# High and low parts of the input weights kept in DRAM between the two halves of the tokens

## The chip, the cores and the metric

The kernel runs on one core of one Trainium2 chip. The metric is the device time of one execution in microseconds (us). Smaller is better. A NeuronCore has a matrix engine (TensorE, PE, with its weight loads as PEld), three engines for element-wise work (VectorE DVE, ScalarE ACT, GpSimd POOL), and DMA engines; nearly all DMAs of this kernel are issued on the queue of SyncE (SP).

## The reference

One layer of a hybrid decoder over 1024 prompt tokens and 8 single sample tokens, width 1024. Cut to what matters here:

```python
def parallel_mixer(h, shift0, wkv0, w_in, ...):
    proj = h @ w_in                    # 1024 -> 2816 columns
    z_a = gelu(proj[..., :1024])       # u, v of mixer A (4 heads x 128)
    out_a = chunk_spatial_gate(u, headnorm(v), gm_ws, gm_bs)
    pb, shift_new = token_shift(proj[..., 1024:], shift0, mu)
    r, k, v, wl, al, gl = split(pb)    # mixer B: 8 heads x 64, and three lora inputs
    yb, wkv_new = wkv7_scan(r, decay, k, v, kk, a, wkv0)   # a recurrence over the tokens
    out_b = (headnorm(yb) + bonus) * g
    return concat([out_a, out_b]) @ w_out, ...

def layer(x):
    x = x + parallel_mixer(rmsnorm(x), ...)
    x = x + cross_attn(rmsnorm(x), mem_k, mem_v, w_xq, w_xo)
    x = x + square(relu(rmsnorm(x) @ w_up)) @ w_down
```

Everything is float32. The 2816 columns of `w_in` are 22 blocks of 128 columns.

## The kernel before

**Products.** A float32 product is made of three matmuls in the format fp32r: each operand is split into a high part (the value cast to fp32r) and a low part (the value minus that), and high x high, high x low and low x high are summed in PSUM (`gemm`, L125). `split` (L100) is a cast on ACT (L103) and a subtraction on DVE or POOL (L104).

**First phase.** The mixer runs in two halves of tokens (`hf` 0 and 1): 512 prompt tokens and the 8 sample tokens, then 512 prompt tokens. In each half, every one of the 22 column blocks is projected once: `proj` (L358) loads the 1024 x 128 block as a tile `wst` (512 KB, in rows of 512 bytes; `w_tile`, L109), splits it into `wh` and `wl` (`load_w`, L114), multiplies it with the halves `xh`, `xl` of the normalised x in two blocks of columns, 48 matmuls in all, and scales the result out of PSUM on DVE (L369). So each block of `w_in` is loaded and split twice. The subtraction runs on DVE or POOL by a rule in L361: in the first half 8 on DVE and 14 on POOL, in the second 14 on DVE and 8 on POOL. `rkv`, `loras` (by way of `shifted`) and `proj_a` call `proj`.

The tags `wst`, `wh` and `wl` belong to the pool `wp` (L90) with two buffers each, so a weight tile is loaded at most two projections ahead of its split, and split at most two ahead of its matmuls. `wst` has other users: the x of the second half as it is read and turned (`x_store`, L278), that x again at the start of the second half (`load_x`, L314), the memory tokens (`mem_norm`, `mem_load`) and the weights of all later stages.

Beside the projections the first phase runs the recurrence of mixer B for pairs of heads in chunks of 64 tokens (`decay`, `factors`, `gram`, `inverse`, `join`, `fold`, `chain`, `outs`, `gn`), mixer A (`norm_a`, `mix_a`), the sample tokens, and at its end the keys and values of the memory (`memkv`, 16 weight blocks loaded and split like the others). A list written by hand (`ORDER`, L39) sets the order in which these steps are written down. From it and from a model of the times the compiler sets the order of the instructions on each engine and queue; each engine and queue then takes its own in that order, and waits on semaphores.

**Second phase.** Output projection, cross attention and the feed-forward layer, from about 665 us on. It doesn't use the projections' code.

Of the kernel before, what the change touches and what calls it, by code (L numbers as in the profile page):

```python
# [9 lines left out]
F32 = mybir.dt.float32  # L10
F32R = mybir.dt.float32r
# [8 lines left out]
P = 128  # L20
D = 1024
KT = 8
# [48 lines left out]
class K:  # L71
    ORDER = order()

    def __init__(self, ctx, tc, a, o, phases=9, dbg=None):
        self.ctx, self.tc, self.nc, self.a, self.o = ctx, tc, tc.nc, a, o
        self.dbg = dbg or {}
        nc = self.nc
        self.consts = ctx.enter_context(tc.tile_pool(name="consts", bufs=1))
        self.dr = ctx.enter_context(tc.tile_pool(name="dr", bufs=1, space=DRAM))
        self.cp = ctx.enter_context(ExitStack())  # L80
        self.pg = self.cp.enter_context(tc.tile_pool(name="pg", bufs=2, space=PSUM))
        self.pm = self.cp.enter_context(tc.tile_pool(name="pm", bufs=2, space=PSUM))
        self.d_o = [self.dr.tile([8, P, HALF], F32, name=f"d_o{i}") for i in range(2)]
        self.d_os = self.dr.tile([8, P, NB], F32, name="d_os")
        self.d_x = self.dr.tile([8, P, T], F32, name="d_x")
        self.d_h = self.dr.tile([16, 7, P, HT], F32, name="d_h")
        self.d_m = self.dr.tile([P, KT, NMEM], F32, name="d_m")
        self.d_k = self.dr.tile([8, P, NMEM], F32, name="d_k")
        self.d_v = self.dr.tile([NMEM, D], F32, name="d_v")
        self.wp = ctx.enter_context(tc.tile_pool(name="wp", bufs=2))  # L90
        with ExitStack() as c1:
            self.phase1(c1)
        if phases >= 2:
            self.phase2(phases)
# [141 lines left out]
    def phase1(self, c1):  # L236
        nc, tc = self.nc, self.tc
        self.sb, self.sa, self.xp, self.s1 = (c1.enter_context(tc.tile_pool(name=nm, bufs=1)) for nm in ("sb", "sa", "xp", "s1"))
        self.s2a, self.s2 = (c1.enter_context(tc.tile_pool(name=nm, bufs=2)) for nm in ("s2a", "s2"))
        self.sl = c1.enter_context(tc.tile_pool(name="sl", bufs=1, side="right"))  # L240
        self.pc = c1.enter_context(tc.tile_pool(name="pc", bufs=1, space=PSUM))
        self.py = c1.enter_context(tc.tile_pool(name="py", bufs=2, space=PSUM))
        self.pre, self.prew, self.scales = [], [], []
        first = [t[2] + 12 if t[0] == "loras" else t[2] + 4 * t[3] for t in self.ORDER if t[0] in ("loras", "rkv")]
        for i in range(4):
            xt = (self.sa if i < 2 else self.sb).tile([P, D], F32, tag=("zv", "zv", "pt", "nb")[i], name="xt", bufs=2 if i < 2 else 1)
            nc.sync.dma_start(xt, self.a["x_prompt"][0][i * P:(i + 1) * P, :])
            self.pre.append(xt)
            if i % 2 == 1:
                self.prew.append(self.w_tile(self.a["w_in"][0][:, 1024 + first[i // 2] * P:1024 + (first[i // 2] + 1) * P]))  # L250
        self.ident = self.consts.tile([P, P], F32, name="ident")
        make_identity(nc, self.ident)
        self.g = {}
        self.prm = self.consts.tile([P, 74], F32, name="prm")
        self.params([("norm_mix_g", 8)], self.s1.tile([64, P], F32, tag="xsr", name="prm_g"), 0)
        self.params([("tshift_mu", 14)], self.s1.tile([P, P], F32, tag="strow", name="prm_mu"), 8)
        self.half = ({}, {})
        self.nb = None
        for name, *args in self.ORDER:
            if args and name not in ("memkv", "sample_update"):  # L260
                self.s = self.half[args[0]]
            getattr(self, name)(*args)
# [95 lines left out]
    def proj(self, hf, col0, dst, sdst):  # L358

        nc, tc = self.nc, self.tc  # L360
        w = self.load_w(self.a["w_in"][0][:, col0:col0 + P], st=self.prew.pop(0) if self.prew else None, eng=nc.vector if hf == int(col0 >= 1024) else nc.gpsimd)  # L361
        for b0, b1 in ((0, 256), (256, self.ncols(hf))):
            ps = self.pg.tile([P, 512], F32, tag="g", name="ps_g")
            self.gemm(ps[:, 0:b1 - b0], w, self.s["xh"], self.s["xl"], slice(b0, b1))
            if self.scales:
                self.scales.pop(0)()
            e = min(b1, HALF)
            with tc.high_priority():
                nc.vector.tensor_tensor(dst[:, b0:e], ps[:, 0:e - b0], self.s["rb"][:, b0:e], op=ALU.mult)  # L369
                if b1 > HALF:  # L370
                    nc.vector.tensor_tensor(sdst, ps[:, HALF - b0:b1 - b0], self.s["rb"][:, HALF:], op=ALU.mult)

    def shifted(self, hf, mi, out):

        nc, s1, s2 = self.nc, self.s1, self.s2
        raw = s2.tile([P, HALF + 1], F32, tag="raw", name="raw")
        if hf == 0:
            nc.gpsimd.memset(raw[:, 0:1], 0.0)
        else:
            nc.scalar.copy(raw[:, 0:1], self.carry[:, mi:mi + 1])  # L380
        self.proj(hf, 1024 + mi * P, raw[:, 1:], self.sraw[:, :, mi])
        nc.gpsimd.tensor_copy((self.carry if hf == 0 else self.shp)[:, mi:mi + 1], raw[:, HALF:HALF + 1])
        nc.scalar.activation(out, raw[:, 1:], AF.Copy, scale=self.mu1[:, mi:mi + 1])
        nc.vector.scalar_tensor_tensor(out, raw[:, 0:HALF], self.g["tshift_mu"][:, mi:mi + 1], out, op0=ALU.mult, op1=ALU.add)
# [1278 lines left out]
```

## Time and profile before

| | us |
|---|---|
| median of 3 runs | 1791.45 (1782.59 to 1793.16) |
| the profiled execution, its own time | 1794.84 |
| its span, first to last instruction | 1793.1 |
| PE busy in the span | 1634.6 (91%) |
| DVE, POOL, ACT busy | 1221.3, 837.1, 781.1 |

The profile is of one execution. Busy time is time in which an engine executes something; issuing and waiting are not counted. PE's matmuls are pipelined, and the ends of them are modelled, so that a busy PE may still be below its peak. A wait is put down to the instruction that ended it. L12 is line 12 of the kernel before. The span began with the first instruction, and all times of rows are counted from there.

### The profile page before, as it was taken

What the parts mean: (1) busy time and instruction counts of PE and PEld (TensorE: products, weight loads), DVE (VectorE), ACT (ScalarE), POOL (GpSimd) and SP (SyncE); (2) the same over time, 40 slices, a digit from 0 to 9 for tenths busy, and PEclk for the clock granted to TensorE, in tenths of its full rate; (3) what the DMA queues carried; (4) which work ended last, traced back from release to release, by engine and by line L of the source; (5) the groups of instructions that cost most, each with busy time, mean ns of one, the idle gap of its engine ahead of it and who ended that gap; (6) DMA issues with size and microseconds to landing.
All of it is one profiled execution on the core that took longest, in us unless ns stands there. A gap on an engine that the chain in (4) does not pass through costs nothing. (4 is left out here: it accounts for less than half of the span.)

```text
span 1793.1 us, 38347 instructions
## 1 busy us (share of the span) xinstructions
PE 1634.6 (91%) x15379; PEld 1521.9 (85%) x15379; DVE 1221.3 (68%) x2300; ACT 781.1 (44%) x1467; POOL 837.1 (47%) x643
## 2 busy tenths in 40 slices
PE   6989868998897689998999889999999999999997
PEld 6878757886786578887988789999999989999997
DVE  5586687768757965656667365655655697877796
ACT  4535543455443234433344233444544564444442
POOL 5450152323146864466343178687754533222343
PEclk8999978999898889999999999999999999999998
DMA  4411423221122456555455342567644585555442
GB/s 139 118 37 58 124 69 93 83 57 52 53 76 73 131 172 196 174 169 175 144 184 165 139 130 82 167 201 225 195 155 142 186 281 184 156 142 153 137 125 107
DMA packets 248547, 244.28 MB, mean 136 GB/s; under 512 B 24937, under 2 KB 191233, under 8 KB 248369
## 3 DMA queue, kind: packets, MB, share of 16 engines
q1 hardware_dynamic: 248324, 241.82, 44.1%
q8 instruction: 121, 1.98, 0.5%
q14 instruction: 58, 0.47, 0.1%
q10 hardware_dynamic: 44, 0.01, 0.0%
HBM read 179.95 MB, written 61.83 MB: 135 GB/s over the span
## 5 line engine op out<-in xcount | busy, mean ns | idle before, releaser
L104 POOL TENSOR_TENSOR wl<-wst,wh 128x1024 fp32r<-128x1024 f32 x70 | 170.3, 2433 | 125.6 <-ACT wh L103 112.1
L1215 PE MATMUL ps_S<-c_o,wS 128*128 128x258 f32 x1536 | 226.4, 282 | 0.0
L1215 PE MATMUL ps_S<-c_cb,wS 128*128 128x258 f32 x1536 | 226.0, 282 | 0.0
L136 PE MATMUL ps_g<-xh,wh 128*128 128x256 f32 (+1 forms) x704 | 214.6, 305 | 5.4 <-ACT xr L288 1.8
L136 PE MATMUL ps_g<-xl,wh 128*128 128x256 f32 (+1 forms) x704 | 209.6, 298 | 0.5 <-DVE xl L104 0.5
L136 PE MATMUL ps_g<-xh,wl 128*128 128x256 f32 (+1 forms) x704 | 207.7, 296 | 0.0
L1215 PEld LDWEIGHTS ps_S<-c_cb,wS 128*128 128x128 f32 x1536 | 201.8, 189 | 0.0
L1215 PEld LDWEIGHTS ps_S<-c_o,wS 128*128 128x128 f32 x1536 | 201.8, 189 | 0.0
L136 PE MATMUL ps_g<-o,wh 128*128 128x260 f32 (+1 forms) x768 | 178.0, 325 | 14.5 <-DVE yq L1240 8.9
L1215 PE MATMUL ps_A<-c_cb,wA 128*128 128x258 f32 x1152 | 173.0, 284 | 7.6 <-ACT c_cb L103 3.9
L1215 PE MATMUL ps_A<-c_o,wA 128*128 128x258 f32 x1152 | 172.7, 284 | 0.0
L1215 PEld LDWEIGHTS ps_A<-c_cb,wA 128*128 128x128 f32 x1152 | 153.4, 190 | 8.8 <-ACT c_cb L103 4.3
L1215 PEld LDWEIGHTS ps_A<-c_o,wA 128*128 128x128 f32 x1152 | 153.2, 190 | 0.4 <-DVE c_o L104 0.4
L103 ACT CAST wh<-wst 128x1024 fp32r<-128x1024 f32 x92 | 96.1, 1046 | 130.5 <-PE ps_g L136 63.9
L136 PEld LDWEIGHTS ps_g<-o,wh 128*128 128x128 f32 x768 | 129.2, 191 | 27.6 <-issue 9.2
L136 PEld LDWEIGHTS ps_g<-xh,wh 128*128 128x128 f32 x704 | 140.3, 199 | 12.9 <-issue 5.0
L136 PEld LDWEIGHTS ps_g<-xl,wh 128*128 128x128 f32 x704 | 139.9, 199 | 5.6 <-issue 2.2
L136 PEld LDWEIGHTS ps_g<-xh,wl 128*128 128x128 f32 x704 | 139.2, 198 | 3.0 <-issue 1.4
L1171 POOL TENSOR_TENSOR rS<-wr,rS 128x512 f32<-128x512 f32 x48 | 70.4, 1467 | 121.9 <-DMA wr<-in_w_down_dram 61.7
L136 PE MATMUL ps_g<-o,wl 128*128 128x260 f32 (+1 forms) x384 | 123.5, 322 | 1.4 <-POOL wl L104 1.4
L103 ACT CAST wS<-rS 128x512 fp32r<-128x512 f32 x96 | 59.3, 620 | 144.1 <-POOL rS L1171 84.1
L104 DVE TENSOR_TENSOR wS<-rS,wS 128x512 fp32r<-128x512 f32 x96 | 81.9, 853 | 46.6 <-ACT wS L103 46.3
(493 smaller groups left out, 3877.2 us busy)
## 6 DMA issues: line engine op xcount, KB each, us to landing
hb<-d_h SPq DMA_DIRECT2D x105, 258.0 KB
wst<-in_w_in_dram SPq DMA_DIRECT2D x44, 512.0 KB
d_h<-ht SPq DMA_DIRECT2D x64, 258.0 KB
wr<-in_w_down_dram SPq DMA_DIRECT2D x26, 512.0 KB
d_h<-yq SPq DMA_DIRECT2D x48, 258.0 KB
wst<-in_w_out_dram SPq DMA_DIRECT2D x16, 512.0 KB
ck<-in_cache_mem_k_dram SPq DMA_DIRECT2D x32, 256.0 KB
ck<-in_cache_mem_v_dram SPq DMA_DIRECT2D x32, 256.0 KB
```

Of the source, the lines that this page charges most:

```text
L103: (heng or nc.scalar.copy)(hi, src)
L104: (eng or nc.vector).tensor_tensor(lo, src, hi.bitcast(F32), op=ALU.subtract)
L136: nc.tensor.matmul(ps, l[:, k, :], r[:, cols], start=(k == 0 and i == 0), stop=(k == kt - 1 and i == 2))
L1171: nc.gpsimd.tensor_tensor(R[n], R[x], R[y], op=op)
L1215: nc.tensor.matmul(ps[:, s], l[:, i, :], r[:, c, cols], start=k == 0 and j == 0, stop=k == 3 and j == 2)
```

## The change

In the first half `proj` loads and splits as before, and when the matmuls are written down it stores both halves of the weights, as they stand in SBUF, to a new DRAM tensor `d_w` (22 blocks, high and low, 512 KB each; a partition's 4 KB are one row). In the second half it makes no split: it loads the two halves from `d_w` into tiles `w2`. These take, in turn, the buffers of (`wh`, `wl`), of (`wh`, `wl`) again, and both buffers of `wst`.

```diff
+        self.d_w = self.dr.tile([22, 2, P, KT, P], F32, name="d_w")
...
-        self.pre, self.prew, self.scales = [], [], []
+        self.pre, self.prew, self.scales, self.nw = [], [], [], 0
...
     def proj(self, hf, col0, dst, sdst):
-        w = self.load_w(self.a["w_in"][0][:, col0:col0 + P], st=self.prew.pop(0) if self.prew else None, eng=nc.vector if hf == int(col0 >= 1024) else nc.gpsimd)
+        if hf == 0:
+            w = self.load_w(self.a["w_in"][0][:, col0:col0 + P], st=self.prew.pop(0) if self.prew else None, eng=nc.vector if hf == int(col0 >= 1024) else nc.gpsimd)
+        else:
+            tags = (("wh", "wl"), ("wh", "wl"), ("wst", "wst"))[self.nw % 3]
+            self.nw += 1
+            w = [self.wp.tile([P, KT, P], F32R, tag=tg, name="w2") for tg in tags]
+            for j in range(2):
+                nc.sync.dma_start(w[j].bitcast(F32), self.d_w[col0 // P, j])
...
+        if hf == 0:
+            for j in range(2):
+                nc.sync.dma_start(self.d_w[col0 // P, j], w[j].bitcast(F32))
```

## Rows read from the trace of the kernel before

**Rows 1.** The page's first part: busy us, share of the span, instructions of each engine

```profile
PE 1634.6 (91%) x15379; PEld 1521.9 (85%) x15379; DVE 1221.3 (68%) x2300; ACT 781.1 (44%) x1467; POOL 837.1 (47%) x643
```

**Rows 2.** Stages: length, busy of PE, PEld, DVE, ACT, POOL, clock, DMA share, GB/s

```profile
0.00:310.00 310.00, 257.08 (x3075) 227.27 (x3075) 215.81 (x497) 145.92 (x267) 117.92 (x152) 0.89 0.31 90
310.00:556.00 246.00, 229.65 (x2520) 197.99 (x2520) 176.86 (x437) 117.80 (x230) 78.71 (x67) 0.94 0.21 64
556.00:665.00 109.00, 72.37 (x1190) 63.56 (x1190) 88.37 (x161) 33.94 (x60) 81.55 (x64) 0.80 0.48 139
```

**Rows 3.** PE's waits in 310 to 556: us in total, times, longest

```profile
PE psgate L705 <- ACT y L702: 4.9, 1, 4.9
PE ps_j L584 <- DVE pt L567: 3.6, 1, 3.6
PE psf L624 <- ACT bk L547: 2.3, 1, 2.3
...
PE psz L646 <- ACT bk L626: 1.1, 1, 1.1
```

**Rows 4.** PE's waits in 556 to 665

```profile
PE psgn L700 <- DVE y L671: 10.7, 1, 10.7
PE psf L624 <- DVE y L671: 9.5, 1, 9.5
```

**Rows 5.** Weight splits in 310 to 556: busy us, mean ns, idle before and why

```profile
L103 ACT CAST wh<-wst 128x1024 fp32r<-128x1024 f32 x22 | 23.0, 1045 | 25.8 <-PE ps_g L136 22.4 <-DMA wst<-in_w_in_dram 1.7 <-issue 1.6
L104 DVE TENSOR_TENSOR wl<-wst,wh 128x1024 fp32r<-128x1024 f32 x14 | 18.8, 1340 | 2.2 <-ACT wh L103 2.2
L104 POOL TENSOR_TENSOR wl<-wst,wh 128x1024 fp32r<-128x1024 f32 x8 | 20.2, 2527 | 39.9 <-ACT wh L103 39.9
```

**Rows 6.** Timeline of SP's issues: start us, us, queue, line

```profile
12.11 0.33 SPq L847 DMA_DIRECT2D bsb<-in_gm_bs_dram  x1
...
13.03 0.44 SPq L713 DMA_DIRECT2D strow<-in_state_shift_dram  x1
...
46.16 1.01 SPq L111 DMA_DIRECT2D wst<-in_w_in_dram  x2
...
303.87 3.75 SPq L315 DMA_DIRECT2D xr<-d_x  x2
310.51 9.95 SPq L111 DMA_DIRECT2D wst<-in_w_in_dram  x4
```

**Rows 7.** Timelines of DVE and POOL around the second half's first weight subtraction

```profile
315.18 0.60 DVE L864 TENSOR_SCALAR vn<-vn,bnmv,lnrs 128x128 f32<-128x128 f32 x2
...
316.30 2.56 DVE L864 TENSOR_SCALAR vn<-vn,bnmv,lnrs 128x128 f32<-128x128 f32 x2
...
316.07 2.44 POOL L104 TENSOR_TENSOR wl<-wst,wh 128x1024 fp32r<-128x1024 f32 x1 [7.82 <-ACT wh L103]
```

**Rows 8.** Windows with DMA share and GB/s last; the last: matmuls of L136 alone

```profile
1009.00:1022.00 13.00, 8.60 (x32) 6.93 (x33) 1.95 (x5) 1.21 (x3) 0.74 (x1) 0.87 0.80 296
46.00:60.00 14.00, 13.94 (x107) 12.60 (x106) 6.09 (x16) 7.52 (x11) 6.98 (x9) 1.00 0.52 152
...
46.00:160.00 114.00, 75.57 (x547) 70.39 (x546) 0.94 0.26 75
```

**Rows 9.** Timelines of ACT, POOL and PE: casts, subtractions, matmuls

```profile
37.15 2.00 ACT L103 CAST wh<-wst 128x1024 fp32r<-128x1024 f32 x2 [15.74 <-issue]
50.48 1.06 ACT L103 CAST wh<-wst 128x1024 fp32r<-128x1024 f32 x1
...
308.18 1.33 ACT L106 ACTIVATE xh<-xr,prm 128x512 fp32r<-128x512 f32 x2 [0.94 <-DMA xr<-d_x]
...
38.27 2.35 POOL L104 TENSOR_TENSOR wl<-wst,wh 128x1024 fp32r<-128x1024 f32 x1 [0.37 <-ACT wh L103]
...
48.14 0.28 PE L136 MATMUL ps_g<-xh,wl 128*128 128x264 f32 x1
...
316.69 0.58 PE L136 MATMUL ps_g<-xh,wh 128*128 128x256 f32 x1
```

## What the change was predicted to do

> **What bounds the kernel now.** I read the busy times first: TensorE (PE) is busy 91% of the span, no other engine over 68% [rows 1]. The change touches only the projections, so I cut the span by stage next [rows 2]: first half of the tokens 0 to 310 us, second half 310 to 556, the tail of that half (recurrence, memory keys and values) 556 to 665, the rest after. The reader is to see how little PE idles where the splits are taken away: 246 - 229.65 = 16.4 us in the second half, 109 - 72.37 = 36.6 us in the tail. Then PE's waits in these two stretches [rows 3, 4]. The first names no wait for `wh` or `wl`. It names copies and vector work of the recurrence (4.9 us for an ACTIVATE of `gn`, 3.6 us for `inverse`, 2.3 us for `ends`); the tail's largest, 10.7 and 9.5 us, are for `y` out of `outs`. So the second half is bound by PE's own work, the tail by the recurrence's chain over VectorE (DVE), ScalarE (ACT) and GpSimd (POOL). The splits sit beside both.
>
> **What it removes.** In the second half 22 casts on ACT, 23.0 us; 14 subtractions on DVE, 18.8 us; 8 on POOL, 20.2 us [rows 5]. PE waits for none of them by name, so they don't come off the time one for one. They count only through what stands behind them on in-order engines. I price this by bounds: nothing below; above, all PE idle time of the second half and half that of the tail (the other half stands behind copies of `memkv` and `inverse` that stay), 16.4 + 18.3 = 34.7 us. The removed work is 18.8 of 176.9 us of DVE's time and 23.0 of 117.8 us of ACT's [rows 2, 5], 11 and 20%. I let PE's waits shrink by 15% in the second half, 2.5 us, and by the 11% of DVE in the tail, 4.0 us, since only what arrives earlier can help there. One more place: the first projection of the second half. Its x halves are done early, but its weight tile `wst` shares two buffers with the x loads, so that its load is issued at 310.51, after the last x load [rows 6], and its subtraction runs on POOL from 316.07 to 318.51 [rows 7], while PE begins with the high part at 316.69 and then turns to the recurrence [rows 9]. Read back into `wh` and `wl`, free since the projections before, these weights can be there first: I take 2.0 us, out of the waits of 2.3 and 1.1 us there [rows 3]. Sum of the gains: 8.5 us.
>
> There is a second effect of POOL's subtractions. Beside the one at 316.07 DVE needs 2.56 us for two ops whose like took 0.60 us just before [rows 7]: some 2 us lost. Over 8 subtractions that is at most 16 us of DVE time, which again is off PE's list; by the 11% for 18.8 us it would be worth another 3 us at most. I leave it to the range.
> The Trainium skill, "SBUF — State Buffer", section "Who interferes with whom", states that a VectorE op with two SBUF inputs is blocked for the whole of a GpSimd op that reads SBUF. The trace agrees that DVE is held up, here even for an op with one large input. By that rule the gain would be the 8.5 us and these 3 us, so 11.5 us.
>
> **What it adds in the first half.** 44 stores of 512 KB on SP's queue, 23 MB. An SP issue takes 0.33 to 0.5 us [rows 6]; 44 are about 18 us of a queue that mostly waits. No row shows a store of this shape. The nearest are transfers with rows of 4 KB: a window of them moved 296 GB/s at a share of 0.80 [rows 8], 370 GB/s at full share. So a pair of 1.05 MB needs an estimated 2.8 us, all 22 need 62 us, or 0.20 of the 310 us; the stage's share is 0.31 [rows 2]. There is room on average. At the busiest place, 46 to 60 us, the share is 0.52 [rows 8]; the 107 matmuls there, 48 a projection, are some two projections; they add 2.1 MB, 5.7 us of 14, 0.41: 0.93, tight but below full.
>
> The stores also hold `wh` and `wl`. Each has two buffers, so the cast of projection n+2 waits for the matmuls of n, and now for its stores too. ACT works in order: behind a late cast stand all its copies for the recurrence, and POOL's subtraction, and then PE. The tightest case is the third projection: subtraction done at 38.27 + 2.35 = 40.6, last matmul issued at 48.14 and over at 48.4 [rows 9], so that the stores have 7.8 us to land; the pair needs 2.8 us and the delay of a landing. For that delay an x load gives a bound: it was issued at 303.87 [rows 6] and ended a wait of ACT at 308.18 [rows 9], 4.3 us for 512 KB. 2.8 + 4.3 = 7.1 us is still below 7.8. I price the hold at nothing; its cover is the matmuls, and if that is gone it costs what the rival below says. What I do charge: at 46.16 SP issues two loads at once [rows 6], and the cast at 50.48 follows [rows 9]. The stores of the two projections whose casts run at 37.15 [rows 9] come due at the same time; with half of their 2.1 MB ahead of these loads they land 2.8 us later, and PE has nothing else there. Low end 0, high end 5.7; I take 2.0 us, somewhat less than that delay, since the split that follows ends a little before PE wants it.
>
> **What it moves.** Loads of the second half: 22 of 512 KB become 44 of 512 KB. At 2.8 us a pair [rows 8] that is 62 us of transfer in 246, 0.25, in a stage whose share is 0.21 with the old loads in it [rows 2]. A projection's tiles come free when the one three before it ends; between lie two projections of 48 matmuls, at the 107 matmuls in 14 us of the dense stretch [rows 8] 12.6 us in all, against 7.1 us for a pair to land. Nothing. SP waits now for PE where it waited for the subtraction; behind it stand small loads and `d_o` stores that have no reader near by. The three sets of buffers also hold both `wst` each third time; until `mem_load` nobody else wants them. Nothing.
>
> **Sum.** 8.5 - 2.0 = 6.5 us less. The profiled execution took 1794.8 us (span 1793.1 and 1.7 around it); 1788.3 then. It lies 3.4 us over the median of the runs, 1791.45, so I predict 1785.
>
> **Rivals.**
> *The recurrence is freed.* If the waits in [rows 3, 4] are mostly for engines that the splits held up, the upper bound comes off: 34.7 less 2.0 us, 1759. For it: DVE is busy 88.37 of the tail's 109 us, POOL 81.55 [rows 2]. Against it: the work removed lies before the tail, and the tail's own load stays. 18%.
> *The stores hold the tiles.* Slower. The place is the first half from 46 to 160 us, where 547 matmuls [rows 8], 11 projections, run close together. It decides once a pair lands more than 7.8 us after the subtraction: the share of 0.93 has only to be uneven for that. Price one store late or both, 1.4 to 2.8 us, for each of 11, 15 to 31 us, less 6.5: 1791.45 + 9 to 1791.45 + 24, 1800 to 1816, about 1808. The Trainium skill, "DMA: Bandwidth & Descriptors", section "Anatomy of one DMA", says, of DMAs issued from GpSimd, that a completion waits for the receipt of the write, the longer when the target is HBM; no row here shows a store's landing. 15%.
> *The order is drawn anew.* SP issued a load of `strow` at 13 us [rows 6], whose step, `sample_shift`, stands in the middle of the written list for this half: the order on each queue is set at compile time and not by the text. With 66 more transfers and 44 fewer vector instructions the engines' order can differ anywhere in the first 665 us. One wait like the two of 10 us in the tail more, and the gain is gone: 1791.45 - 6.5 + 10 = 1795, no change. 17%.
> *Forecast*: 50%, itself 1774 to 1797.
>
> **Numbers.** A measurement of this kernel can tell about 1% from no change, 18 us. Faster by more, below 1773.5: the freed recurrence nearly whole and a little of the forecast, 0.20. Slower by more, above 1809.4: not quite half of the held tiles, some of the new order, and what of the forecast's costs I may have missed, 0.13. Within: 0.67. The range is 1760 to 1809: it reaches to the freed recurrence's full price and over the middle of the held tiles, and leaves out about a tenth at each end.
>
> **What would show it.** Right: the cast and subtraction groups in the second half gone; PE's waits in the first half unchanged but for 2 us near 50; the second half ending some 4 us earlier counted from its start, the tail 4 us shorter; no wait of ACT for a DMA on `d_w`. Wrong: ACT or POOL waiting for `d_w` stores in the first half; PE waiting for `w2` loads; the tail shorter by over 15 us, or a wait of PE that isn't in [rows 3, 4].

## The result and the profile after

The changed kernel takes 1804.25 us (median of 7 executions, 1799.04 to 1814.14), the kernel before, run beside it, 1790.79 us (7, 1782.59 to 1793.16): ratio 1.0076, 95% interval 1.0051 to 1.0101. It is 13.5 us slower, inside the predicted range and on the other side of the forecast of 1785.

The profiled execution of the changed kernel was its longest, 1814.14 us, 9.9 us over the median, with a span of 1812.4 us; that of before was 1794.84 us. The two profiles therefore differ by 19.3 us, and the places of the loss below are those of these two executions. From here on lines are those of the changed kernel (L104 of before is L105, L498 is L509, L607 is L618, L816 is L827).

Busy us, share of the span and instructions of each engine, against [rows 1]:

```profile
PE 1649.6 (91%) x15379; PEld 1532.2 (85%) x15379; DVE 1198.9 (66%) x2286; ACT 754.5 (42%) x1442; POOL 806.2 (44%) x635
```

The splits are gone: ACT has 27 us less work, DVE 22, POOL 31. The stages, in the columns of [rows 2]:

```profile
0.00:310.00 310.00, 252.54 (x2961) 222.29 (x2962) 209.07 (x481) 142.15 (x263) 115.21 (x150) 0.88 0.50 165
310.00:556.00 246.00, 234.49 (x2584) 201.07 (x2583) 155.06 (x430) 93.91 (x205) 49.06 (x59) 0.94 0.31 107
556.00:665.00 109.00, 63.61 (x961) 54.18 (x960) 90.41 (x155) 29.19 (x58) 70.27 (x58) 0.75 0.40 118
```

The second half has PE at 234.49 us for 229.65 before: it idles less in this window, as hoped. The tail has 63.61 for 72.37, at a granted clock of 0.75 for 0.80, although ACT and POOL do less there. PE's waits in the tail, against [rows 4]:

```profile
PE ps_j L595 <- DVE pt L578: 12.9, 1, 12.9
PE psgram L509 <- DVE ab L510: 11.8, 1, 11.8
PE ps_kvt L1008 <- DVE kvt L1003: 8.9, 3, 7.4
PE psf L635 <- DVE y L682: 7.0, 1, 7.0
```

The wait of 10.7 us for `y` of before is gone; 12.9 us for the end of `inverse` and 11.8 us for `gram` stand in its place. Place by place, from the first and last matmuls in PE's timeline: the first half's last projection ends 7.1 us later (312.6 for 305.5), the second half's 5.3 us later (561.3 for 556.0), and the last matmul of `join 1 1` 23.8 us later (682.5 for 658.7). So the stretch from the last projection to the end of that join is 18.5 us longer (121.2 for 102.7); some 4 us of it come back later.

Within that stretch two pieces grew most; 3.2 us more stand ahead of them. The *ladder* of `inverse 1 1` is 28 small DVE operations between two transposes, from 607.9 to 634.1 us before (26.3 us) and from 616.4 to 651.1 after (34.7). The *join* behind it, from its first matmul to its last, is 637.9 to 658.7 before (20.8 us) and 654.8 to 682.5 after (27.7). In both kernels the four `sample_update` steps, each of six POOL and three DVE operations and eleven loads, run beside them. The timelines show what they do. First DVE's and POOL's rows in the ladder (start, us, engine, line, tiles), the first of them from the kernel before, where no POOL operation ran beside it:

```profile
633.90 0.21 DVE L564 TENSOR_TENSOR pb<-pb,ptmp 128x28 f32<-128x28 f32 x1
...
644.99 2.27 DVE L575 TENSOR_TENSOR pb<-pb,ptmp 128x72 f32<-128x72 f32 x1
...
649.62 0.20 DVE L574 TENSOR_TENSOR ptmp<-pb 128x28 f32<-128x28 f32 x1
649.85 1.21 DVE L575 TENSOR_TENSOR pb<-pb,ptmp 128x28 f32<-128x28 f32 x1
...
644.82 2.33 POOL L105 TENSOR_TENSOR wl<-wst,wh 128x1024 fp32r<-128x1024 f32 x1
...
649.74 1.26 POOL L826 TENSOR_TENSOR stmp<-sS,sbv 128x512 f32<-128x512 f32 x1 [0.22 <-DMA sbv<-d_sv]
```

The operation that took 0.21 us before takes 1.21 us when it starts just behind a POOL product of 1.26 us, and a larger one of its kind 2.27 us behind a weight subtraction of 2.33. Over 0.9 us took 13 of the 28, and 9 before; every one of these has a POOL operation beside it. All 28 together take 23.3 us, for 16.7 before. Then SP, POOL, DVE and PE in the join:

```profile
659.60 9.25 SPq L815 DMA_DIRECT2D sbv<-d_sv  x8
...
661.45 1.27 POOL L818 TENSOR_TENSOR stmp<-sS,sbv 128x512 f32<-128x512 f32 x1 [10.46 <-DMA sbv<-d_sv]
...
673.71 1.27 POOL L826 TENSOR_TENSOR stmp<-sS,sbv 128x512 f32<-128x512 f32 x1
...
672.07 1.58 PE L616 MATMUL ps_j<-tt,ab 32*32 32x32 f32 x64
...
675.01 0.69 DVE L827 TENSOR_REDUCE sy<-stmp 128x8 f32<-128x512 f32 x1 [6.89 <-POOL stmp L826]
675.73 0.68 DVE L618 COPY wj<-ps_j 32x512 f32<-32x512 f32 x1
...
676.47 0.31 PE L622 MATMUL ps_j<-wj,dt 32*32 32x32 f32 x2 [2.27 <-DVE wj L618]
...
681.32 1.19 PE L622 MATMUL ps_j<-wj,dt 32*32 32x32 f32 x62
```

DVE waits 6.89 us for the last product of the last `sample_update`, whose first product had itself waited 10.46 us for a load, and behind this reduction stands the copy of `wj` that the join needs. In the compiled order of the kernel before the last reduction stands behind all copies of the join; in the changed kernel it stands right in front of that one. The 6.89 us aren't the price, though: what the copy reads, the matmuls of L616, is ready only at 672.07 + 1.58 = 673.65 us. The copy starts at 675.73, so that it is about 2 us late, and PE waits 2.27 us for it. After that PE runs 25 matmuls of `memkv` between the first two and the other 62 of L622; in the kernel before such a block stands ahead of all 64 and runs while the copy is made. From the end of L616 to the end of the join it takes 8.9 us for 4.3 before, from the join's start to there 18.9 for 16.5. So the late copy is some 2 of the join's 6.9 us; the rest lies in the order of PE's matmuls and in its other waits.

### The profile page after: what moved, and what is told of

Read it like the earlier page. It is cut to its first block, busy times and chain, and to the rows that moved or that the text cites. A ratio compares the mean times of both kernels' runs of the same rounds, so it can differ in the third digit from the quotient of the medians.

```text
span 1812.4 us, 38412 instructions
## 1 busy us (share of the span) xinstructions
PE 1649.6 (91%) x15379; PEld 1532.2 (85%) x15379; DVE 1198.9 (66%) x2286; ACT 754.5 (42%) x1442; POOL 806.2 (44%) x635
## 5 line engine op out<-in xcount | busy, mean ns | idle before, releaser
L105 POOL TENSOR_TENSOR wl<-wst,wh 128x1024 fp32r<-128x1024 f32 x62 | 149.3, 2408 | 106.4 <-ACT wh L104 94.5
L137 PE MATMUL ps_g<-xh,w 128*128 128x256 f32 x704 | 148.6, 301 | 1.4 <-DVE raw L377 1.4
L137 PEld LDWEIGHTS ps_g<-xh,w 128*128 128x128 f32 x704 | 116.1, 197 | 8.8 <-issue 3.4
L104 ACT CAST wS<-rS 128x512 fp32r<-128x512 f32 x96 | 59.2, 620 | 145.4 <-POOL rS L1182 85.9
L104 ACT CAST wh<-wst 128x1024 fp32r<-128x1024 f32 x70 | 73.1, 1045 | 111.0 <-PE ps_g L137 63.2
L105 DVE TENSOR_TENSOR wS<-rS,wS 128x512 fp32r<-128x512 f32 x96 | 81.6, 850 | 50.6 <-ACT wS L104 50.4
L137 PE MATMUL ps_g<-xh,wh 128*128 128x256 f32 (+1 forms) x352 | 108.5, 309 | 5.7 <-ACT xr L289 2.2
L137 PE MATMUL ps_g<-xl,wh 128*128 128x256 f32 (+1 forms) x352 | 106.5, 303 | 0.6 <-DVE xl L105 0.5
L137 PE MATMUL ps_g<-xh,wl 128*128 128x256 f32 (+1 forms) x352 | 105.3, 300 | 0.0
L137 PE MATMUL ps_g<-xl,w 128*128 128x256 f32 x352 | 104.8, 298 | 0.0
```

The source lines that it names most:

```text
L104: (heng or nc.scalar.copy)(hi, src)
L105: (eng or nc.vector).tensor_tensor(lo, src, hi.bitcast(F32), op=ALU.subtract)
L137: nc.tensor.matmul(ps, l[:, k, :], r[:, cols], start=(k == 0 and i == 0), stop=(k == kt - 1 and i == 2))
```

## The experiments

All ratios are to the kernel before, run on the same chip beside each kernel (its medians lay at 1790.8 to 1792.5 us). The table has, beside the ratio, when the last projection of each half ends, how long ladder and join are and when the join ends, each from the timelines of the one profiled execution. The ratios are not the quotients of the medians given in the text; the two differ by up to 0.15%. The profiled execution is the slowest of its kernel for the changed kernel and before_update_early, the fastest for after_late2 and after_update_dve. From the end of the join to the end of the span it takes from 1116 to 1147 us (1134 before, 1130 changed), so that the columns don't give the time by themselves.

| kernel | ratio (95%) | half 1 ends | half 2 ends | ladder | join | join ends |
|---|---|---|---|---|---|---|
| before | 1 | 305.5 | 556.0 | 26.3 | 20.8 | 658.7 |
| changed | 1.0076 (1.0051 to 1.0101) | 312.6 | 561.3 | 34.7 | 27.7 | 682.5 |
| stores_only | 1.0072 (1.0041 to 1.0104) | 309.2 | 564.7 | 30.2 | 22.6 | 665.6 |
| loads_only | 1.0047 (1.0019 to 1.0075) | 304.3 | 555.3 | 26.7 | 29.8 | 670.0 |
| two_sets | 1.0081 (1.0051 to 1.0111) | 308.2 | 549.2 | 35.0 | 30.5 | 672.6 |
| before_swap2 | 0.9956 (0.9918 to 0.9994) | 297.7 | 541.6 | 29.6 | 22.2 | 662.3 |
| before_swap3 | 1.0047 (1.0021 to 1.0072) | 307.9 | 567.6 | 30.6 | 22.4 | 674.9 |
| before_swap6 | 0.9982 (0.9951 to 1.0012) | 304.6 | 553.8 | 27.6 | 19.7 | 655.6 |
| after_swap2 | 1.0046 (1.0025 to 1.0067) | 301.3 | 546.9 | 29.4 | 29.4 | 665.5 |
| before_no_update | 0.9950 (0.9922 to 0.9978) | 306.1 | 556.6 | 21.9 | 22.0 | 651.6 |
| after_no_update | 0.9940 (0.9922 to 0.9958) | 310.4 | 555.3 | 21.6 | 19.5 | 651.1 |
| update_early | 0.9952 (0.9924 to 0.9980) | 309.1 | 562.4 | 20.7 | 13.6 | 652.0 |
| before_update_early | 1.0047 (1.0025 to 1.0068) | 308.4 | 616.9 | 25.4 | 15.0 | 660.1 |
| early_few_stores | 0.9999 (0.9982 to 1.0016) | 304.1 | 558.6 | 21.4 | 23.0 | 658.0 |
| early_act_queue | 0.9974 (0.9950 to 0.9999) | 306.5 | 561.4 | 22.2 | 18.7 | 656.7 |
| early_swap2 | 0.9978 (0.9955 to 1.0002) | 301.4 | 552.9 | 18.4 | 23.3 | 647.6 |
| after_update_dve | 1.0083 (1.0057 to 1.0110) | 308.7 | 549.7 | 35.6 | 24.0 | 678.8 |
| after_late3 | 1.0049 (1.0022 to 1.0076) | 310.2 | 555.5 | 31.4 | 20.0 | 664.3 |
| after_late2 | 1.0081 (1.0051 to 1.0110) | 311.4 | 553.6 | 26.0 | 16.9 | 654.4 |
| before_late2 | 0.9994 (0.9974 to 1.0013) | 304.1 | 554.7 | 23.9 | 21.5 | 655.9 |

### One half of the change alone, one buffer rule, one list

**stores_only**: in `proj`, the branch for `hf == 1` taken out again.

```diff
-        if hf == 0:
-            w = self.load_w(...)
-        else:
-            ... loads from d_w
+        w = self.load_w(...)
```

> First half as in the changed kernel (44 stores to d_w), second half as in the kernel before (loads of w_in and splits); d_w is written and never read. Theory A, the stores themselves cost (SP's queue, held tiles, bandwidth): the end of the first half's last projection, 305.5 us before and 312.6 after, stays near 312, and the whole takes 1797 to 1803. Theory B, the order drawn anew costs, wherever its waits happen to fall: the first half is late by some other amount, 0 to 8 us, and the tail (1790.8 before) decides; any time from 1788 to 1810. Theory C, the loss comes from the loads of the second half: the whole takes 1790 to 1794.

It took 1805.86 us, 0.72% over before, as much as the whole change. Its tail is about as long as before (100.9 us for 102.7 from the last projection to the end of the join, ladder and join 52.8 for 47.1); its loss lies ahead of the tail, 3.7 us at the end of the first half and 8.7 at the end of the second, where its work is that of before. Theory C falls; theory A is missed too, by the end of the first half (309.2 for 312) and by the time (at most 1803), and only theory B's wide range holds it.

**loads_only**: two pairs stored, all loads from these.

```diff
-        if hf == 0:
+        if hf == 0 and self.nst < 2:
             for j in range(2):
-                nc.sync.dma_start(self.d_w[col0 // P, j], ...)
+                nc.sync.dma_start(self.d_w[self.nst, j], ...)
+            self.nst += 1
...
-                nc.sync.dma_start(w[j].bitcast(F32), self.d_w[col0 // P, j])
+                nc.sync.dma_start(w[j].bitcast(F32), self.d_w[self.nw % 2, j])
```

> Second half as in the changed kernel (44 loads from DRAM, no casts, no subtractions), but in the first half only two of 22 pairs are stored, and all loads read these two, so that the output isn't the reference's; the work and the shapes of the transfers are the same. Theory A: the gain that was predicted is there, the first half ends at 305.5 as before, and the whole takes 1781 to 1786. Theory B: the second half is shorter, but the tail can be longer by 5 to 15 us; 1785 to 1800. Theory C: 1800 to 1806, as the full change.

1800.61 us, 0.47% over before, where theories B and C meet: theory A's gain isn't there. Its first half is that of before and its second ends where that of before ends; the join is 9.0 us longer. The two halves of the change, 0.72 and 0.47%, add up to 1.19% for the 0.76% of the change. Their intervals are too wide to tell from this whether each cost belongs to its part.

**two_sets**: `tags = ("wh", "wl")` for every projection of the second half.

> The full change, but the loads of the second half go to the buffers of wh and wl alone, never to both wst. If the third set (two wst held at the turn by the x loads) makes the projection after the turn late, 14.6 us at its end in the changed kernel, this one is late by 3 to 5 us there and the whole takes 1792 to 1798. If it is the clock or the x loads themselves, the second projection of the second half stays late by 12 us or more, and the whole is within 4 us of 1804.

It fits neither theory whole: 1807.99 us is what the second one has, the end of the second projection what the first one has. That projection ends 4.5 us later than before (348.2 for 343.7; 14.6 later in the changed kernel), and the second half even ends 6.8 us earlier; ladder and join are 65.5 us long and eat it all.

**before_swap2**: two words of the list exchanged, `decay 0 0` and `kknorm 0 1`.

> The kernel before with two neighbours of the written list exchanged (kknorm 0 1 before decay 0 0); the work is the same, the compiled order differs on every engine from the fifth projection on. Theories A and C: the order by itself is worth little, within 4 us of 1790.8. Theory B: the time moves by more than 5 us, either way, without any work added.

1786.79 us, 0.44% less than before, for the same work (5.2 us between the medians). So the time moves by 5 to 8 us when the order alone is compiled anew. **before_swap3** and **before_swap6** exchange `rkv 0 3 1` with `proj_a 0 0 1`, and `gn 0 2` with `values 1 0`:

> The kernel before with rkv 0 3 1 and proj_a 0 0 1 exchanged in the list; same work, the compiled order differs from TensorE's matmul 1002 on (some 130 us). If the order before was the best of many, this is slower: 1792 to 1806, with a longer tail. If an exchange is as likely to gain, 1778 to 1790. Within 2 us of 1791 would speak against the order as a cause.

> The kernel before with gn 0 2 and values 1 0 exchanged; same work, the order differs only from TensorE's matmul 2871 on, in the second half. First half as before, its last projection ending at 305.5; the tail decides: 1792 to 1806 if the order before was the best of many, 1778 to 1790 if an exchange is as likely to gain.

1800.54 us (+0.47%) and 1790.49 us (-0.18%, not to be told from none). Three exchanges gave a gain, a loss and nothing, between -0.44 and +0.47%: without any added work an effect of half a per cent can be had. The change's 0.76% is more than any of the three, but its interval overlaps with that of before_swap3 (1.0021 to 1.0072).

**after_swap2**: the change on the list of before_swap2.

> The change made on the kernel whose list has kknorm 0 1 before decay 0 0 (1786.8 us without the change, 0.44% below before). If the change costs by itself, this is 13 us slower than that, 1798 to 1802. Theory B, the order drawn anew decides: anything from 1783 to 1808, and ladder and join, 29.6 and 22.2 us without the change, come out at other lengths.

1798.64 us, 0.9% over before_swap2 by the ratios (0.66% by the medians). With this list, too, the change loses, and again the join is long, 29.4 us for 22.2, with an equal ladder.

### The sample_update steps taken out of the tail

**before_no_update** and **after_no_update**: `sample_update 0` to `3` struck from the list, `ys` set to zero.

> The kernel before without the four sample_update steps (their states and the samples' outputs are not computed); they are 24 vector operations on GpSimd and 12 on VectorE, 40 loads, nearly all of them between 580 and 680 us. Theory D, the tail's length is set by how these steps fall on the ladder of inverse 1 1 and on the join behind it: the ladder, 26.3 us long before, comes down to some 15 us and the join from 20.8 to 18, and the whole is 10 to 15 us shorter than before, 1776 to 1782. Rival: the tail waits for the weights of memkv; then not more than 4 us come off.

> The changed kernel without the four sample_update steps, as above. Theory D: ladder and join, 34.7 and 27.7 us in the changed kernel, come down to the same 15 and 18 us as in the kernel before without them, 25 to 30 us off; the whole takes 1776 to 1786, no more than 4 us from the other. Rival, the stores and the turn make the loss: the whole stays 10 to 14 us above the other.

1780.86 and 1781.94 us, ratios 0.995 and 0.994: the two kernels are alike. The changed one loses 22 us by it, the other 10. Ladder and join are 43.9 and 41.1 us; the second half ends at 556.6 and 555.3, the join at 651.6 and 651.1. The sizes expected (15 and 18 us) were too small, since the subtractions for `memkv` still meet the ladder: each of the three operations over 0.9 us in either kernel stands beside one. The join of the kernel before isn't shortened at all (22.0 us for 20.8). (The steps' loads are 44, not the 40 of the expectation.) The tail's windows (as above; the first kernel before, then the changed one, both without the steps):

```profile
556.00:665.00 109.00, 76.96 (x1241) 65.08 (x1240) 77.03 (x158) 39.18 (x73) 55.19 (x42) 0.83 0.27 81
```

```profile
556.00:665.00 109.00, 79.02 (x1264) 67.80 (x1264) 77.39 (x160) 39.81 (x73) 55.55 (x42) 0.80 0.29 87
```

PE is busy 77 and 79 us there, for 72.37 and 63.61 with the steps. So without these steps the change loses nothing and gains nothing, although its first half still ends 4.3 us later (310.4 for 306.1). That points to the steps' meeting with the tail as the place of the loss. It is one pair, though, and to strike the steps compiles the order anew as well, which alone was worth up to 0.47%.

**update_early**: two_sets, and the steps moved into the second half of the list, behind `sample_a`, `rkv 1 2 0`, `rkv 1 3 0` and `proj_a 1 1 0`. Their tiles, in the kernel before in buffers of `r`, `raw` and `k`, go to the now unused `wst`.

```diff
-        S = s2.tile(S64, F32, tag="r", name="sS")
+        st = self.wp.tile([P, 2, NB, 64], F32, tag="wst", name="sSt")
+        S, tmp, bb = st[:, 0], st[:, 1], []
...
-            b = s2.tile(S64, F32, tag="raw", name="sbv")
+            if i % 2 == 0:
+                bb.append(self.wp.tile([P, 2, NB, 64], F32, tag="wst", name="sbv"))
+            b = bb[-1][:, i % 2]
...
-        tmp = s2.tile(S64, F32, tag="k", name="stmp")
```

> The changed kernel with two sets of buffers, so that both wst are free in the second half, and the four sample_update steps moved there, their tiles in wst; all work is done. Theory D: the tail loses ladder and join as above, 15 to 25 us against the two-set kernel (1808), and the steps cost PE little in the second half, where GpSimd is busy 57 of 246 us: 1783 to 1793, so perhaps faster than before. Rival: GpSimd's operations hold VectorE up in the second half instead, the last projection ends 8 us later and the whole takes 1798 or more.

1784.37 us, 0.9952 (0.9924 to 0.9980): with all work done it is faster than both kernels. The gain over the kernel before, 0.48%, is no more than an exchange in the list gave (0.44%); the step from two_sets, 1.3%, is. Its stages:

```profile
0.00:310.00 310.00, 253.86 (x3047) 223.24 (x3049) 214.24 (x486) 143.57 (x264) 116.26 (x150) 0.88 0.51 166
310.00:556.00 246.00, 228.48 (x2494) 197.22 (x2491) 167.16 (x436) 92.95 (x203) 81.89 (x82) 0.94 0.41 136
556.00:665.00 109.00, 81.84 (x1293) 70.18 (x1291) 79.43 (x166) 39.84 (x76) 57.12 (x45) 0.83 0.27 80
```

POOL is now busy 81.89 us in the second half (57.42 in two_sets), and PE idles 17.5 us there for 11.5 in the changed kernel; in the tail PE's work goes from 63.61 to 81.84 us. The last projection ends as late as in the changed kernel (562.4), the join 30.5 us earlier.

**before_update_early**: the same move and tiles, on the kernel before.

> The kernel before (splits in both halves, nothing stored) with the sample_update steps moved to the same place and tiles as in the kernel with the updates early, which took 1784.4 us with the change. In the kernel before the two wst buffers carry every weight load of the second half, so that the updates' tiles stand between them. If it is the buffers and engines freed by the change that make room for the move, this one is not faster than 1788 and its last projection ends later than 562 us. If moving the steps out of the tail is all, this one is at 1774 to 1782, faster than with the change by what the stores cost.

1798.28 us, 0.47% slower: the last projection ends at 616.9 us. The steps' tiles and the weights of the second half queue for the same two buffers: in front of the steps' loads SP waits up to 15.3 us for a split. With these tiles the move pays only where the change has freed the buffers; other buffers for it in the kernel before weren't tried.

**early_few_stores**, **early_act_queue** and **early_swap2**: update_early with two pairs stored (as in loads_only), with the stores on `nc.scalar`, and with the list of swap2.

> The kernel with the updates early, with two of the 22 pairs stored and read back for all (the output isn't the reference's). The 42 stores cost what this one is faster: theory A (the stores' queue and holds make the first half 3.6 us late and the turn more) 4 to 9 us less, 1775 to 1780; if the first half's lateness is regained later, within 3 us of 1784.4, although the first half ends at 305 us and not at 309.

> The kernel with the updates early, with the 44 stores issued on ScalarE's queue and not on SP's. If SP's waits in front of the stores (91 us for casts in the changed kernel) delay the loads behind them, the last projection of the first half comes 2 to 4 us earlier than 309 and the whole takes 1778 to 1782. If the stores cost nothing there, within 3 us of 1784.4; if ScalarE's own waits for the subtractions hold its copies up, 1787 or more.

> The kernel with the updates early, with kknorm 0 1 before decay 0 0 in the list. With the tail's bound gone the order of the first half should show less: theory D within 4 us of 1784.4. Theory B: the second half ends at another time, 540 to 565 us, and the whole follows it, 1774 to 1792.

1792.24 (0.9999), 1790.58 (0.9974) and 1787.79 us (0.9978). The first is a miss of both theories: 42 stores less, a first half that ends 5.0 us earlier, and the whole 0.47% slower than update_early; its join is 23.0 us long, not 13.6. The second, with the stores off SP, has the first half's end 2.6 us earlier, as expected, but the time isn't: it lies where the expectation put a hold-up of ScalarE's copies, and ScalarE's waits in front of the casts don't show one (31.7 us in the first half, for 31.4 in update_early). early_swap2 is level with update_early within what these intervals tell. So what the stores cost stays open: stores_only is 0.72% slower than before, but here taking them away gains nothing.

### How the steps make the tail long

**after_update_dve**: the six POOL operations of `sample_update` written with `nc.vector`.

> The changed kernel with the six GpSimd operations of each sample_update step put on VectorE (24 in all). Hold-up theory: with GpSimd left to the weights' subtractions, only 3 to 5 of the ladder's 28 operations take over 0.9 us, not 13; their sum falls from 23.3 to 12 or 13 us, although VectorE has 24 operations of about 0.7 us more, 17 us; the tail gets shorter, the whole 1790 to 1800. Queue theory: the operations stay slow or the added 17 us lengthen ladder and join; 1804 to 1815.

Both theories are half right. The hold-up is there: with these steps off POOL 4 of the ladder's 28 operations take over 0.9 us, not 13, their sum is 13.3 us, not 23.3, and three of the four left stand beside a weight subtraction. DVE and POOL of this kernel:

```profile
645.49 0.25 DVE L574 TENSOR_TENSOR ptmp<-pb 128x100 f32<-128x100 f32 x1
...
646.76 2.09 DVE L574 TENSOR_TENSOR ptmp<-pb 128x88 f32<-128x88 f32 x1
...
646.33 2.42 POOL L105 TENSOR_TENSOR wl<-wst,wh 128x1024 fp32r<-128x1024 f32 x1 [3.21 <-ACT wh L104]
```

But the other work that DVE does inside the ladder grows from 8.5 to 19.2 us, the ladder stays at 35.6 us, and the kernel takes 1807.81 us. So the ladder is as long with the steps on either engine: on POOL they hold DVE's operations up, on DVE they stand between them. (The profile is of the fastest of ten executions, 1796.84 us.)

**after_late3** and **after_late2**: the state tile of the last step, or the last two, in the buffer that the join's `dt` has, so that they come behind the join. **before_late2** does the latter to the kernel before.

```diff
-        S = s2.tile(S64, F32, tag="r", name="sS")
+        S = self.sb.tile(S64, F32, tag="ta", name="sS") if pr >= 3 else s2.tile(S64, F32, tag="r", name="sS")
```

> The changed kernel, with the state of the last sample_update step in the buffer that the join's dt has, so that this step comes behind the join; the compiled order shows its reduction behind the join's copies, as in the kernel before. If the reduction in front of the copy of wj costs what the profiles show, the wait of 6.89 us on VectorE goes, the join comes down from 27.7 to 20 to 23 us, and the whole takes 1795 to 1800. If the join is long because of the weights of memkv or the low clock, it stays over 26 us and the whole within 3 us of 1804.

1797.87 us, as expected, 6.4 us less than the changed kernel; the join is 20.0 us. The copy of `wj` waits for its matmuls alone:

```profile
660.13 0.68 DVE L618 COPY wj<-ps_j 32x512 f32<-32x512 f32 x1 [0.79 <-PE ps_j L616]
```

The wait of 6.89 us is gone, and the join is 7.7 us shorter. But the reduction had made the copy only some 2 us late; with the new order all 64 matmuls of L622 stand behind those of `memkv` again, and the second half of this profile ends 5.8 us earlier (555.5 for 561.3). So what the reduction alone is worth isn't shown. Medians 6.4 us apart, with intervals that overlap (1.0022 to 1.0076, 1.0051 to 1.0101), don't prove that the whole move gains either.

> The changed kernel, with the last two sample_update steps behind the join. The ladder meets fewer of GpSimd's operations: its length comes down from 34.7 to 22 to 27 us and the join to 20 to 23; the whole takes 1783 to 1792, as the kernel before or a little faster. If something later waits for the steps (the samples' outputs), the gain is given back: 1796 or more.

> The kernel before with the same move of the last two steps. If with the tail's order equal the change is worth nothing, this one is within 4 us of the changed kernel with the move. If the change costs by its stores, this one is 5 us or more faster; if removing the splits gains, 5 us or more slower.

before_late2 is level with before, 1792.70 us. In the profile of after_late2 ladder and join are as short as expected (26.0 and 16.9 us) and the join ends at 654.4. But the median is 1807.07 us, while the profiled execution took 1794.05, the shortest of its six. In that profile the output projection's first cast, `o<-ost`, starts at 707.7 us for 678.4 before (702.9 in before_late2): I take it that the steps put off behind the join hold it up, and that part of the gain is given back there; no run shows it, and the changed kernel has this cast at 701.0. Why the two kernels' medians are 14 us apart and their spans 1.2 us, the runs don't show. The change costs 0.87% in this pair, although ladder and join are no longer with it (42.9 us for 45.4). By the expectation that is the case of a cost outside the tail, in the stores, and stores_only says the same; so the tail isn't the whole of the loss.

## Why the prediction was wrong

**Gains in the second half (4.5 us of 8.5).** The size isn't shown, and at the end it was worth nothing. From the end of the first half to the end of the second half the changed kernel takes 248.7 us for 250.5, after_no_update 244.9 for 250.5 and two_sets 241.0, but loads_only 251.0, and after_swap2 245.6 for 243.9 in before_swap2. The exchanges alone have this stretch between 243.9 and 259.7 us. What comes out early there waits in the tail: two_sets ends its projections 6.8 us before the kernel before and its join 13.9 us after it.

**The first projection of the second half (2.0 of these).** The weights are there first, as forecast: their loads were issued at 289.02 us. The step failed at what comes next. The matmuls waited for something else, `rs`, whose place in DVE's order is behind `vn`:

```profile
PE ps_rb L299 <- DVE rs L151: 2.2, 1, 2.2
```

The profiles of the changed kernel, loads_only, two_sets, after_no_update and update_early have this wait (1.8 to 3.6 us), those of before, stores_only and before_swap3 don't, nor does after_swap2, so that it hangs on the list too. Between 320 and 330 us PE idled 3.0 us in the changed kernel, and from 345 us on its clock was low: here two windows, the clock third from last; before it was 1.00 in both.

```profile
345.00:350.00 5.00, 5.00 (x26) 4.48 (x25) 3.26 (x13) 2.23 (x5) 1.27 (x1) 0.50 0.15 56
350.00:355.00 5.00, 5.00 (x22) 4.32 (x22) 1.12 (x4) 0.21 (x1) 0.00 (x0) 0.50 0.01 2
```

At 0.50, the lower level of 1.2 GHz, the next projection took 14.4 us for 7.6. That the idle time brought the clock down is not shown: between the two the clock stood at 1.00 (335 to 340 us), and the kernel before, whose PE idled 3.4 us from 310 to 320, had 1.00 from 320 to 365; its first windows:

```profile
310.00:315.00 5.00, 2.72 (x70) 2.56 (x71) 3.85 (x20) 3.98 (x8) 0.00 (x0) 0.63 0.52 158
315.00:320.00 5.00, 3.87 (x43) 3.27 (x40) 5.00 (x10) 2.62 (x4) 3.45 (x2) 0.68 0.32 92
320.00:325.00 5.00, 4.76 (x27) 3.13 (x26) 4.68 (x15) 1.55 (x5) 2.50 (x2) 1.00 0.77 223
```

I had looked at who waits for the weights, not at what is late next.

**The tail (4.0).** This is the step that failed: 4.0 us shorter was forecast, 18.5 us longer was measured, from the last projection to the end of the join. I put the tail's waits down to the chain of the recurrence, and let them shrink by DVE's share of the removed work, 11%. But the removed work lies ahead of the tail, as I wrote against the first rival, and so nothing in the tail is shortened by it; ladder and join of the pair without the updates are 43.9 and 41.1 us. In the tail ladder, join, `memkv` and four `sample_update` steps meet, and in the changed kernel they met worse: 62.4 us of ladder and join for 47.1. The waits of 12.9 and 11.8 us that grew there aren't among [rows 4], the sign that I had set down for being wrong.

**POOL holding DVE up.** I left it to the range, up to 3 us in the second half. The mechanism is right, the place wrong: it costs in the tail, where POOL's work was not removed. The Trainium skill, "SBUF — State Buffer", section "Who interferes with whom", states that a DVE instruction with two SBUF inputs contends with a GpSimd instruction that reads SBUF, and that the lock on the ports they share is exclusive. The rows agree: started 0.17 us behind a subtraction of 2.33 us, DVE's operation took 2.27.

**Costs of the first half (2.0).** The bandwidth was right: the share went from 0.31 to 0.50 (0.20 more were worked out), and at 46 to 60 us to 0.91, for 0.93:

```profile
46.00:60.00 14.00, 13.94 (x107) 12.60 (x106) 5.87 (x14) 7.45 (x10) 6.52 (x8) 1.00 0.91 301
```

The cast at 50.48 us came at 52.49, 2.0 us later as priced, but the projection behind it still ended at 62.9 for 63.0, so that this cost nothing. The hold of `wh` and `wl` at nothing was right: no engine's wait is put down to a store, and the first twelve projections end within 0.5 us of before. What I didn't look at is where the stores would stand in SP's queue: it waits in front of them for casts, 91.1 us over the half (waited for: total, times, longest):

```profile
SPq L382 <- ACT wh L104: 91.1, 17, 15.2
```

But SP waited before as well, and all its waits in this half add up to 237 us, for 267 before, so that this row by itself shows no cost. From the 13th projection on the first half is late, by 1.4 to 7.1 us: the term of 2.0 us was too small, at the end even its high end of 5.7, and its place was wrong. stores_only has 3.7 us of it and loads_only none, so it comes with the stores; whether from the queue, or from the order, the runs don't settle.

**What it moves.** Priced at nothing, and nothing it cost: in the changed kernel PE never waits for a load from `d_w` (POOL has two waits put down to one, 9.1 and 1.3 us), and two_sets, which leaves both `wst` alone, isn't faster.

**The rivals.** The recurrence wasn't freed; the tiles weren't held. The third rival, at 17%, came nearest: the order drawn anew, more waits in the tail. It failed by its price, one wait of 10 us less my gain of 6.5. There was no gain to set against it, and the tail had two places that could grow, by 8.4 and 6.9 us. The three exchanges in the list, a gain, a loss and nothing, show that such a move can go either way without any change of the work, which speaks for more than 17%. That 1804 lies inside the range is luck: the range reached there for the tiles that the stores would hold, and they held none.

**What stays open.** Of the pairs that differ by the change alone, three lose 0.8 to 0.9% (the change itself, on swap2's list, and with two steps late) and one is level (no updates). With the updates early the kernel with the change is 0.95% faster than the one without, but these two differ by two_sets as well, and the one without is held up by its buffers. That the loss is bound to the updates in the tail is suggested by the level pair and by update_early, and not shown: stores_only and the pair with two steps late lose 0.7 to 0.9% with a tail about as long as without the change, and the join varies from 13.6 to 23.3 us even where the steps are early. What the stores cost, and what the order alone, the runs don't separate; the order lies in the compiler's model, which no run opens.

## What to carry to other kernels

Work taken off engines that don't bound a stage brought nothing here. The time that it freed became worth something when work from a later stage was moved into the gap, four small steps: 0.8% slower became 0.5% faster (0 to 0.3% in three variants of it). Where a compiler orders the instructions, measure first what a meaningless exchange does (here -0.4 to +0.5%) and read every smaller effect against it. Where a late, unimportant instruction stands in front of an urgent one in an engine's queue, price it by when the urgent one's own inputs were ready (2 us here), not by the whole wait (6.89).

## What was unexpected in the hardware

A DVE operation on 128x28 elements took 0.21 us alone and 1.21 us beside a POOL product of 1.26 us; with 13 such meetings the 28 operations of a ladder took 23.3 us, an estimated 16 us more than alone (28 of about 0.25 us). And a projection, part of it for 10 us at a granted clock of 0.50, took 14.4 us for 7.6 with the clock at 1.00; what brought the clock down isn't shown.
